# A list scheduler inside the kernel plans the order of all five queues

## Chip, core and metric

The kernel runs on one core of one Trainium2 chip. The core has five engines with a queue each: TensorE (PE), VectorE (DVE), ScalarE (ACT), GpSimd (POOL) and SyncE (SP), which issues all DMAs here. The metric is the device time of one execution in microseconds; the kernel before took 1773.93, 1771.78 and 1771.08 us in three runs, 1771.78 in the middle.

## What is computed

Two layers of a gated trunk on 640 token columns: 512 latent ones (modulated by `c`, attending to cached context and to themselves) and 128 context ones (modulated by `c_ctx`). Cut to the core, one layer of the reference is:

```python
shift, scale, gate = split(silu(c) @ w_mod + b_mod, 3)
h = rms(x, norm_g) * (1 + scale) + shift
cq, ckv, krope, z_a, qkv_b, ga, gb, z_b, cu, cv, z_c, gl = split(h @ w_in)
o_a = attention(rms(rms(cq) @ w_uq), keys_values(rms(ckv) @ w_ukv, krope))      # 8 heads
o_b = rms(gdn(silu(conv5(qkv_b)), ga, gb, forward) + gdn(..., backward))        # 4 heads, chunked scan
o_c = gelu(cu) * (w_s @ layernorm(gelu(cv)) + b_s)                              # per 128 positions
yb = [(o_a * silu(z_a)) @ w_b0, (o_b * silu(z_b)) @ w_b1, (o_c * silu(z_c)) @ w_b2]
x = x + gate * ((sigmoid(gl) * yb).sum() @ w_o)
```

Beside the two outputs it returns the new ckv, krope and states of the context.

## The kernel before

Activations lie feature-major: 128 features by 640 tokens, worked in two halves of 320 columns. The weights are streamed: a tile `raw` of 128x512 (256 KB, `wload`, L130) is split into a rounded part `hi` by ScalarE (L134) and the rest `lo` by VectorE (L135), and `dense` multiplies in three passes, L146 (hi by hi), L147 and L148 (the two mixed products), into PSUM tiles `dn` of two buffers. Small products go to `mm` (p1, two buffers) and `p2` (two buffers). SBUF tiles are cut from tags with a fixed number of slots (`NB`): `G` has 13, `raw`, `hi` and `lo` 3 each.

Four places matter below.

The start. `Mod.groups` loads the 128x512 tiles of w_mod into `G` (L205) and multiplies them with the two conditioning vectors (L208); after 16 tiles VectorE copies the sums to `mrow` (L210), TensorE transposes them (L213), and out of them come shift and scale of half the features. `make_h` makes with them four of the eight tiles `hh`, `hl` of h, and dense matmuls of layer 0 need these. Then the other 16 tiles follow for the other half. The constants of `late_constants` (L1148), a layer's vectors (`lvec`, L303) and b_mod and norm_g (L190, L192) are small loads.

The scans of the four heads of branch B. Each step multiplies a state, L533 and L534, VectorE corrects (L536), L500 multiplies again, ScalarE weights the result (L505), and L544 makes the state's update. L780 is the spatial product of the gated MLP (branch C), whose input `D` VectorE makes at L701.

The inverses of branch B: small tiled products of 32 and 64 rows in steps; the last joins are L670, L683 and L684.

Attention. `latent_tile` multiplies queries and keys (L1053 with 512 columns, L1054 with 128), `softmax` runs on VectorE and ScalarE (L1040 to L1046), five transpositions follow (L1059), ScalarE copies (L1061) and ten products of 64 rows (L1067) form the output. The preparation of the next pair of heads and the dense blocks of the other branches are laid between by generators.

The order of each queue is set before by the framework: it takes instructions in program order by priority, with its own cost model, and `tc.high_priority(HP)` lifts the splits, the evacuations of `dense`, the softmax and one normalisation above the rest:

```python
with tc.high_priority(HP):
    split_w(w[:, 0:n], hi[:, 0:n], lo[:, 0:n])
```

## Time and profile before

| what | value |
| --- | --- |
| three runs | 1773.93, 1771.78, 1771.08 us |
| span of the profiled execution | 1769.0 us |
| TensorE busy, matmuls | 1719.1 us (97%), 13422 |
| TensorE busy, weight loads | 1573.2 us (89%) |
| VectorE busy | 1075.1 us (61%) |
| ScalarE busy | 817.5 us (46%) |
| DMA, mean share of 16 engines' span | 26% |

The span is that of one profiled execution, and about 3 us shorter than the time of the middle run. Busy shares are means over a program with unlike stages. In the timeline an engine's idle time stands in brackets behind the instruction that ended it, with what released it. Matmuls of plain fp32 are recorded twice each, so that a count of 8 there is four matmuls; L146 to L148 once.

### The profile page before, as it was taken

What the parts mean: (1) busy time and instruction counts of PE and PEld (TensorE: products, weight loads), DVE (VectorE), ACT (ScalarE), POOL (GpSimd) and SP (SyncE); (2) the same over time, 40 slices, a digit from 0 to 9 for tenths busy, and PEclk for the clock granted to TensorE, in tenths of its full rate; (3) what the DMA queues carried; (4) which work ended last, traced back from release to release, by engine and by line L of the source; (5) the groups of instructions that cost most, each with busy time, mean ns of one, the idle gap of its engine ahead of it and who ended that gap; (6) DMA issues with size and microseconds to landing.
All of it is one profiled execution on the core that took longest, in us unless ns stands there. A gap on an engine that the chain in (4) does not pass through costs nothing.

```text
span 1769.0 us, 34645 instructions
## 1 busy us (share of the span) xinstructions
PE 1719.1 (97%) x13422; PEld 1573.2 (89%) x13422; DVE 1075.1 (61%) x3180; ACT 817.5 (46%) x2065; POOL 16.7 (1%) x100
## 2 busy tenths in 40 slices
PE   6999999999999999999999999999999999999999
PEld 3899988898888889999989989888988888899999
DVE  4798888565555643433559988885655656435352
ACT  3466764554544542222335666655544545323231
POOL 0000000000000000000000000000000000000000
PEclk9999999999999999999999999999999999999999
DMA  8211121221112242554432211111211112123224
GB/s 289 70 56 58 54 67 40 67 72 62 40 38 65 63 141 72 167 179 150 156 117 67 61 44 59 59 47 61 72 52 53 50 53 66 62 72 108 78 88 138
DMA packets 86421, 146.37 MB, mean 83 GB/s; under 512 B 14064, under 2 KB 21616, under 8 KB 86256
## 3 DMA queue, kind: packets, MB, share of 16 engines
q1 hardware_dynamic: 86256, 144.15, 26.0%
q8 instruction: 106, 1.74, 0.4%
q14 instruction: 59, 0.48, 0.1%
HBM read 132.28 MB, written 11.83 MB: 81 GB/s over the span
## 4 chain that ended last, share of the span: by engine, by line
PE 85%; DVE 7%; ACT 5%; issue 1%; DMA 1%; SPq 0%; ACTq 0%; DVEq 0%
PE dn L146 19%; PE dn L147 19%; PE dn L148 19%; PE p L1053 3%; PE mm L1067 3%; PE p L1059 2%; DVE C L332 2%; PE p L208 1%; PE mm L500 1%; PE p L147 1%; PE p L148 1%; DVE lo L135 1%; PE p L146 1%; PE mm L544 1%; ACT hi L134 1%
## 5 line engine op out<-in xcount | busy, mean ns | idle before, releaser
L146 PE MATMUL dn<-hh,hi 128*128 128x320 f32 (+1 forms) x2208 | 697.0, 316 | 5.4 <-ACT hh L268 4.9
L147 PE MATMUL dn<-hl,hi 128*128 128x320 f32 (+1 forms) x2208 | 693.0, 314 | 1.2 <-DVE hl L269 1.1
L148 PE MATMUL dn<-hh,lo 128*128 128x320 f32 (+1 forms) x2208 | 693.4, 314 | 0.0
L146 PEld LDWEIGHTS dn<-hh,hi 128*128 128x128 f32 (+1 forms) x2208 | 413.6, 187 | 16.9 <-ACT hh L268 5.9
L147 PEld LDWEIGHTS dn<-hl,hi 128*128 128x128 f32 (+1 forms) x2208 | 413.8, 187 | 6.4 <-DVE hl L269 2.6
L148 PEld LDWEIGHTS dn<-hh,lo 128*128 128x128 f32 (+1 forms) x2208 | 413.7, 187 | 3.7 <-issue 2.2
L135 DVE TENSOR_TENSOR lo<-raw,hi 128x512 fp32r<-128x512 f32 (+1 forms) x326 | 223.9, 688 | 217.6 <-ACT hi L134 212.8
L134 ACT CAST hi<-raw 128x512 fp32r<-128x512 f32 (+1 forms) x326 | 201.2, 619 | 316.6 <-PE dn L147 293.3
L146 PE MATMUL dn<-qkv,hi 128*128 128x320 f32 x384 | 119.7, 312 | 0.0
L147 PE MATMUL dn<-qkv,hi 128*128 128x320 f32 x384 | 119.4, 311 | 0.0
L148 PE MATMUL dn<-qkv,lo 128*128 128x320 f32 x384 | 118.9, 310 | 0.0
L821 ACT ACTIVATE th<-dn 128x320 f32<-128x320 f32 x96 | 41.6, 434 | 110.2 <-PE dn L148 109.8
L1040 DVE TENSOR_REDUCE mx<-p 128x1 f32<-128x640 f32 x64 | 52.6, 822 | 64.2 <-PE p L1054 64.2
L332 DVE SCALAR_TENSOR_TENSOR C<-C,l_conv_w,C 128x644 f32<-128x644 f32 x96 | 84.8, 883 | 5.2 <-ACT C L330 3.4
L1044 ACT ACTIVATE V<-p,mx,scl 128x640 f32<-128x640 f32 x64 | 56.6, 884 | 56.5 <-DVE mx L1042 43.1
L147 PEld LDWEIGHTS dn<-qkv,hi 128*128 128x128 f32 x384 | 72.1, 188 | 0.7 <-issue 0.7
L146 PEld LDWEIGHTS dn<-qkv,hi 128*128 128x128 f32 x384 | 72.1, 188 | 0.7 <-issue 0.7
L148 PEld LDWEIGHTS dn<-qkv,lo 128*128 128x128 f32 x384 | 72.1, 188 | 0.0
L1061 ACT COPY V<-p 128x640 f32<-128x640 f32 x64 | 44.3, 692 | 53.1 <-PE p L1059 53.1
L1053 PE MATMUL p<-G,G 128*128 128x512 f32 x128 | 66.1, 598 | 0.0
L833 DVE SCALAR_TENSOR_TENSOR th<-th,dn 128x320 f32<-128x320 f32 x64 | 31.2, 487 | 44.6 <-PE dn L148 44.6
L1126 DVE SCALAR_TENSOR_TENSOR ya<-dn,gate,ld 128x320 f32<-128x320 f32 (+2 forms) x48 | 19.6, 437 | 54.8 <-DMA ld<-sp 23.0
(395 smaller groups left out, 2675.3 us busy)
## 6 DMA issues: line engine op xcount, KB each, us to landing
raw<-in_w_in SPq DMA_DIRECT2D x244, 256.0 KB, 2.6
G<-in_w_mod SPq DMA_DIRECT2D x96, 256.0 KB, 4.3
raw<-in_w_branch SPq DMA_DIRECT2D x48, 256.0 KB, 2.6
raw<-in_w_o SPq DMA_DIRECT2D x32, 256.0 KB, 2.6
ld<-sp SPq DMA_DIRECT2D x24, 320.0 KB, 3.2
G<-in_w_uq SPq DMA_DIRECT2D x16, 192.0 KB, 2.8
ya<-in_xT SPq DMA_DIRECT2D x8, 320.0 KB, 5.4
sp<-V SPq DMA_DIRECT2D x8, 320.0 KB, 2.5
```

The costliest lines, as they stand in the source:

```text
L134: S.copy(hi, w)
L135: V.tensor_tensor(lo, w, hi, ALU.subtract)
L146: PE.matmul(out, ah, bh, start=start, stop=False)
L147: PE.matmul(out, ah, bl, start=False, stop=False)
L148: PE.matmul(out, al, bh, start=False, stop=stop)
L332: V.scalar_tensor_tensor(cv, buf[:, w : w + 644], convw[:, j, w : w + 1], cv, ALU.mult, ALU.add)
L821: S.activation(ga[c0], acc, AF.Tanh, scale=0.5)
L1040: V.tensor_reduce(mx, src, AX.X, ALU.max)
L1044: S.activation(out, src, AF.Exp, scale=sc_, bias=mx[:, 0:1], accum_out=ls[:, 0:1])
L1053: PE.matmul(psS[:, 0:512], pr.qT[j][:, qs], pr.kT[j][:, 0:512], start=True, stop=True)
L1061: S.copy(pT.rearrange("p a b -> p (a b)"), pst[:, 0:640])
L1067: PE.matmul(po[es, 0:P], pr.Vt[:, kt, e, :] if kt < 4 else pr.Vc[:, e, :], PT[e][:, kt, :], start=(kt == 0), stop=(kt == 4), tile_position ...
```

## The change

Every engine call now goes to a `Recorder`, which notes the operation, the tiles it reads and writes (as sets of columns and partitions) and, from these, what it depends on. No instruction is issued while the program runs. At the end `rec.issue()` lets `plan()` run an event list over all operations: each engine takes, when it is free, the ready operation of lowest priority number (program order, less 100000 under `rec.hp()`); the slots of a tag are given out in program order; costs come from `cost()` and a few constants. Then it issues in the planned order, and each instruction is tied to the one before on its engine and to the last users of its slot. The same tiles and the same 16907 instructions result; the computation is unchanged. In the order after, all rows have the line L330, where `issue()` calls the engine.

```diff
+ENG = {"V": "vector", "S": "scalar", "G": "gpsimd", "PE": "tensor", "SP": "sync"}
+
+TAIL = {"V": 80, "S": 95, "G": 60}
+HOP = {"V": 60, "S": 60, "G": 100, "PE": 60, "SP": 60}
+SLACK = 150
+ISSUE = 55
+DMA_LAG, DMA_RATE = 1900, 250.0
...
+class Recorder:
+
+
+    def __init__(self, tc):
+        self.tc, self.ops, self.off = tc, [], 0
+        self.acc = {}
+        self.tag = {}
+        self.users = {}
+        self.boxes = {}
+        self.rows = {}
...
+    def add(self, eng, meth, args, kw):
+        op = Op()
+        op.n, op.eng, op.meth, op.args, op.kw = len(self.ops), eng, meth, args, kw
+        op.prio = op.n - self.off
+        op.preds, op.succs, op.tiles = set(), [], []
...
+    def cost(self, op, outs, ins):
+        size = lambda x: x.free_size() if callable(x.free_size) else x.free_size
+        e = op.eng
+        op.ld = 0
+        if e == "SP":
+            big = max((x.nbytes() if callable(x.nbytes) else x.nbytes) for x in outs + ins)
+            op.occ, op.lat = ISSUE, big / DMA_RATE
+        elif e == "PE":
+            n = size(outs[0])
+            if op.meth == "transpose":
+                op.ld, op.occ = 107, max(n / 2.4, 64) + 2
+            elif ins[0].dtype == F32R:
+                op.ld, op.occ = 107, n / 2.4 + 13
+            else:
+                rows = ins[0].ap[0][1]
+                op.ld, op.occ = (107, 4 * n / 2.4 + 4) if rows > 64 else (40, 4 * n / 2.4 + 4)
+                if rows > 64:
+                    op.occ = max(op.occ, 120)
+            op.lat = op.occ + 180
+        else:
+            n = max(size(x) for x in outs[:1] + ins[:1])
+            ps = any(self.tag.get(x.tensor.name, ("", False, 0))[1] for x in outs + ins)
+            if e == "V":
+                quick = op.meth in ("tensor_scalar", "tensor_copy", "memset") and not ps
+                d = max(160, 150 + (0.63 if quick else 1.05 * (1 if not ps else 1.0)) * n)
+                if op.meth == "reciprocal":
+                    d = max(160, 150 + 2 * n)
+            elif e == "S":
+                d = max(230, 165 + 0.88 * n) + (190 if "accum_out" in op.kw else 0)
+            else:
+                d = 200 + 1.2 * n
+            op.occ, op.lat = d - TAIL[e], d
...
+        def slots_ok(op, t):
+            for nm in op.tiles:
+                if nm in home:
+                    continue
+                tag = self.tag[nm][0]
+
+                if nxt[tag] != pos[nm] or not any(f[0] <= t for f in free[tag]):
+                    return tag
+            return None
...
+            for s_ in op.succs:
+                s_.left -= 1
+                lag = 0.0
+                if s_.eng != op.eng or op.eng == "SP":
+                    lag = HOP[s_.eng] + (SLACK if s_.eng == "PE" else 0)
+                elif op.eng == "PE":
+                    lag = -1e6
+                s_.ready = max(s_.ready, op.end + lag)
+                if s_.left == 0:
+                    post(s_.ready, "rdy", s_)
+
+        def dispatch(e, t):
+            h = avail[e]
+            if busy[e] > t:
+                return
...
+    def issue(self):
+        out = self.plan()
+        self.rank = {op.n: i for i, op in enumerate(out)}
+        nc = self.tc.nc
+        deps = {}
+        for op, nm in self.slotdeps:
+            deps.setdefault(op.n, []).append(nm)
+        prev = {}
+
+        def behind(op, other, why):
+            info = mybir.DependencyInfo(mybir.DependencyClass.NoSync, mybir.DependencyReason.DATA)
+            self.tc.add_manual_dep(op.ins.ins, other.ins.ins.name, info, reason=why)
+
+        for op in out:
+            op.ins = getattr(getattr(nc, ENG[op.eng]), op.meth)(*op.args, **op.kw)
+            if op.eng in prev:
+                behind(op, prev[op.eng], "order")
+            prev[op.eng] = op
+            for nm in deps.get(op.n, ()):
+                lastof = {}
+                for u in self.users[nm]:
+                    if u.eng not in lastof or self.rank[u.n] > self.rank[lastof[u.eng].n]:
+                        lastof[u.eng] = u
+                for u in lastof.values():
+                    if u.eng != op.eng:
+                        behind(op, u, "slot")
...
+class RecHigh:
+    def __init__(self, rec):
+        self.rec = rec
+
+    def __enter__(self):
+        self.rec.off += HP
+
+    def __exit__(self, *x):
+        self.rec.off -= HP
...
-    V, S, G, PE = nc.vector, nc.scalar, nc.gpsimd, nc.tensor
+    rec = Recorder(tc)
+    V, S, G, PE, SY = (rec.engine(e) for e in ("V", "S", "G", "PE", "SP"))
...
-        nc.sync.dma_start(w[:, 0 : src.shape[1]], src)
+        SY.dma_start(w[:, 0 : src.shape[1]], src)
...
-        with tc.high_priority(HP):
+        with rec.hp():
...
+    rec.issue()
```

All other edits replace `nc.sync` by `SY`, `tc.high_priority` by `rec.hp()` and drop comments.

**At the start, SP's queue**: before, the last of the first 16 w_mod tiles (`G`, of which G_58 is the sixteenth), three raw weights and the next w_mod tiles. The names are tile names with a running number.

```order
L205 DMA G_56_223<-in_w_mod 128x512
L205 DMA G_57_227<-in_w_mod 128x512
L205 DMA G_58_231<-in_w_mod 128x512
L130 DMA raw_73_279<-in_w_small 128x384
L130 DMA raw_76_285<-in_w_in 128x512
L130 DMA raw_79_291<-in_w_in 128x512
L205 DMA G_83_298<-in_w_mod 128x512
L205 DMA G_84_302<-in_w_mod 128x512
```

And after, from the twelfth tile on; between l_gdn and l_kn_rope stand 32 more small loads, which are left out:

```order
L330 DMA G_54_122<-in_w_mod 128x512
L330 DMA G_55_123<-in_w_mod 128x512
L330 DMA raw_73_141<-in_w_small 128x384
L330 DMA raw_76_144<-in_w_in 128x512
L330 DMA raw_79_147<-in_w_in 128x512
L330 DMA l_conv_w_113_181<-in_conv_w 128x60
L330 DMA l_gdn_onorm_114_182<-in_gdn_onorm 128x1
...
L330 DMA l_kn_rope_3060_3128<-in_kn_rope 128x32
L330 DMA G_56_124<-in_w_mod 128x512
L330 DMA G_57_125<-in_w_mod 128x512
L330 DMA G_58_126<-in_w_mod 128x512
L330 DMA G_83_151<-in_w_mod 128x512
```

The 14th to 16th tile (G_56 to G_58) now come behind the raw weights and 35 small loads.

**TensorE's queue at the same place**, before: `p2_36` collects the first half, `p2_82` the second, mm_60 is the transposition, dn_117 and p2_119 the first dense blocks.

```order
L208 MATMUL p2_36_135<-G_57_227,c_s32_13_84 32x256 x2
L208 MATMUL p2_36_135<-G_58_231,c_s32_13_84 32x256 x2
L213 MATMUL mm_60_237<-c_ident_2_69,mrow_59_235 128x128 x2
L208 MATMUL p2_82_297<-G_83_298,c_s32_13_84 32x256 x2
L146 MATMUL dn_117_415<-hh0_62_244,hi_74_281 48x320
L146 MATMUL p2_119_417<-hh0_62_244,hi_77_287 128x320
L208 MATMUL p2_82_297<-G_84_302,c_s32_13_84 32x256 x2
```

And after:

```order
L330 MATMUL p2_36_104<-G_57_125,c_s32_13_81 32x256 x2
L330 MATMUL p2_36_104<-G_58_126,c_s32_13_81 32x256 x2
L330 MATMUL p2_82_150<-G_83_151,c_s32_13_81 32x256 x2
L330 MATMUL mm_60_128<-c_ident_2_68,mrow_59_127 128x128 x2
L330 MATMUL p2_82_150<-G_84_152,c_s32_13_81 32x256 x2
L330 MATMUL p2_82_150<-G_85_153,c_s32_13_81 32x256 x2
L330 MATMUL p2_82_150<-G_86_154,c_s32_13_81 32x256 x2
L330 MATMUL dn_117_185<-hh0_62_130,hi_74_142 48x320
L330 MATMUL dn_118_186<-hh0_62_130,hi_74_142 48x320
```

Four tiles of the second half (G_83 to G_86) are multiplied before the first dense matmul, where one was.

**TensorE in a head's scan**, before: mm_764 and mm_770 are L533 and L534 of two steps, mm_766 is L500, mm_768 L544, dn_842 an L780.

```order
L533 MATMUL mm_764_3776<-Q_757_3759,qkv_418_2046 128x128
L534 MATMUL mm_764_3776<-Q_757_3759,qkv_406_1966 128x128
L780 MATMUL dn_842_4092<-C_807_3913,D_590_2807 128x128
L500 MATMUL mm_766_3782<-Q_765_3779,G_728_3610 128x128
L544 MATMUL mm_768_3787<-Q_767_3784,G_458_2276 128x128
L533 MATMUL mm_770_3791<-Q_763_3774,qkv_418_2046 128x128
L534 MATMUL mm_770_3791<-Q_763_3774,qkv_406_1966 128x128
```

And after, from mm_766 to mm_770:

```order
L330 MATMUL mm_766_834<-Q_765_833,G_728_796 128x128
L330 MATMUL dn_838_906<-hl7_112_180,hi_834_902 128x320
L330 MATMUL dn_838_906<-hh7_111_179,lo_835_903 128x320
L330 MATMUL dn_840_908<-C_807_875,D_578_646 128x128
L330 MATMUL dn_840_908<-C_807_875,D_581_649 128x128
L330 MATMUL dn_840_908<-C_807_875,D_584_652 128x128
L330 MATMUL dn_840_908<-C_807_875,D_587_655 128x128
L330 MATMUL mm_768_836<-Q_767_835,G_458_526 128x128
L330 MATMUL mm_770_838<-Q_763_831,qkv_418_486 128x128
L330 MATMUL mm_770_838<-Q_763_831,qkv_406_474 128x128
```

Two dense matmuls (dn_838) and four L780 (dn_840) have moved between mm_766 and mm_768.

**TensorE in a softmax join**, before: p2_1184 is the score product, p2_1188 the transposition of its softmax, and 23 dense matmuls stand between (five are shown).

```order
L1053 MATMUL p2_1184_5693<-G_1104_5353,G_1075_5195 128x512
L1054 MATMUL p2_1184_5693<-iv_1102_5343,G_1075_5195 128x128
L146 MATMUL dn_1546_7283<-qkv_1478_6895,hi_1544_7279 128x320
L147 MATMUL dn_1546_7283<-qkv_1479_6897,hi_1544_7279 128x320
L148 MATMUL dn_1546_7283<-qkv_1478_6895,lo_1545_7280 128x320
...
L146 MATMUL dn_1554_7323<-hh0_62_244,hi_1549_7313 128x320
L147 MATMUL dn_1554_7323<-hl0_63_245,hi_1549_7313 128x320
L1059 MATMUL p2_1188_5704<-c_ident_2_69,V_1185_5696 128x128 x5
```

And after, with nine L1067 (mm_1172) and twelve products of 256 columns (mm_1183) between, of which some are shown:

```order
L330 MATMUL p2_1184_1252<-G_1104_1172,G_1075_1143 128x512
L330 MATMUL p2_1184_1252<-iv_1102_1170,G_1075_1143 128x128
L330 MATMUL mm_1172_1240<-V_1171_1239,G_1088_1156 64x128
L330 MATMUL mm_1172_1240<-V_1165_1233,G_1088_1156 64x128
L330 MATMUL mm_1172_1240<-V_1171_1239,G_1088_1156 64x128
...
L330 MATMUL mm_1172_1240<-V_1171_1239,Q_1089_1157 64x128
L330 MATMUL mm_1183_1251<-G_1174_1242,C_1031_1099 128x256
L330 MATMUL mm_1183_1251<-G_1175_1243,C_1031_1099 128x256
...
L330 MATMUL mm_1183_1251<-G_1174_1242,iv_1063_1131 128x256
L330 MATMUL p2_1188_1256<-c_ident_2_68,V_1185_1253 128x128 x5
```

The dense matmuls have moved away, and shorter products stand in their place.

## Rows read from the trace of the kernel before

**Rows 1.** The page, parts 1 and 4: busy us (share); chain by engine.
```profile
PE 1719.1 (97%) x13422; PEld 1573.2 (89%) x13422; DVE 1075.1 (61%) x3180; ACT 817.5 (46%) x2065; POOL 16.7 (1%) x100
...
PE 85%; DVE 7%; ACT 5%; issue 1%; DMA 1%; SPq 0%; ACTq 0%; DVEq 0%
```

**Rows 2.** Windows: PE, PEld, DVE, ACT, POOL busy us; clock, DMA share, GB/s.
```profile
0.00:60.00 60.00, 41.44 (x239) 23.53 (x240) 26.05 (x67) 18.32 (x33) 0.54 (x10) 0.91 0.68 228
60.00:260.00 200.00, 197.15 (x1732) 184.87 (x1730) 173.92 (x613) 129.63 (x390) 6.61 (x40) 1.00 0.20 59
260.00:400.00 140.00, 132.76 (x1283) 121.77 (x1284) 98.45 (x334) 74.89 (x218) 1.25 (x3) 1.00 0.20 63
905.00:935.00 30.00, 26.97 (x212) 21.85 (x210) 22.22 (x59) 12.78 (x23) 0.17 (x3) 0.94 0.21 65
1130.00:1270.00 140.00, 132.40 (x1266) 120.79 (x1264) 97.34 (x336) 75.35 (x219) 2.05 (x5) 0.99 0.19 62
1540.00:1769.00 229.00, 225.20 (x1535) 224.85 (x1534) 92.85 (x166) 59.62 (x109) 0.00 (x0) 1.00 0.31 97
```

**Rows 3.** Timeline of SP, start: start us, duration us, line, operation.
```profile
7.18 12.78 SPq L205 DMA_DIRECT2D G<-in_w_mod  x16
20.01 0.42 SPq L130 DMA_DIRECT2D raw<-in_w_small  x1
...
21.48 12.11 SPq L205 DMA_DIRECT2D G<-in_w_mod  x16
```

**Rows 4.** Timeline of SP, 62.5 to 70 us: small loads back to back.
```profile
65.65 0.42 SPq L303 DMA_DIRECT2D l_kv_a_norm<-in_kv_a_norm  x1
...
68.97 0.43 SPq L303 DMA_DIRECT2D l_a_log<-in_a_log  x1
```

**Rows 5.** The page, part 6: count, KB, us from issue to landing.
```profile
raw<-in_w_in SPq DMA_DIRECT2D x244, 256.0 KB, 2.6
```

**Rows 6.** Timeline of PE, start: in brackets idle us before, releaser.
```profile
27.76 0.44 PE L213 MATMUL mm<-c_ident,mrow 128*128 128x128 f32 x2 [0.57 <-DVE mrow L210]
...
31.03 0.63 PE L208 MATMUL p<-G,c_s 128*32 128x256 f32 x4
```

**Rows 7.** Timeline of PE, 294 to 299 us: a head's scan.
```profile
294.25 1.05 PE L780 MATMUL dn<-C,D 128*128 128x128 f32 x8
...
296.69 0.49 PE L500 MATMUL mm<-Q,G 128*128 128x128 f32 x2 [0.22 <-DVE Q L536]
297.70 0.49 PE L544 MATMUL mm<-Q,G 128*128 128x128 f32 x2 [0.52 <-ACT Q L505]
```

**Rows 8.** Line L544: waits before it, by releaser (us, times).
```profile
  ACT Q L505: 8.3, 33
```

**Rows 9.** Line L780: waits before it, by releaser (us, times).
```profile
  DVE D L701: 7.6, 12
```

**Rows 10.** Timeline of PE, 463 to 468 us: one softmax join.
```profile
463.61 0.38 PE L1054 MATMUL p<-iv,G 128*128 128x128 f32 x2
463.75 0.40 PE L146 MATMUL dn<-qkv,hi 128*128 128x320 f32 x1
...
467.06 0.31 PE L147 MATMUL dn<-hl,hi 128*128 128x320 f32 x1
467.29 0.77 PE L1059 MATMUL p<-c_ident,V 128*128 128x128 f32 x5
```

**Rows 11.** Timeline of DVE, 463 to 468 us: the softmax's last step.
```profile
466.68 0.55 DVE L1046 TENSOR_SCALAR V<-V,ls 128x640 f32<-128x640 f32 x1
```

**Rows 12.** Timeline of PE, 454 to 464 us: L1067 and 256-column products.
```profile
459.38 0.98 PE L1067 MATMUL mm<-V,G 128*64 128x128 f32 x13
...
460.62 0.39 PE L147 MATMUL mm<-G,C 128*128 128x256 f32 x1
...
462.63 0.28 PE L148 MATMUL mm<-G,iv 128*128 128x256 f32 x1
```

**Rows 13.** Line L1059: largest wait before it (us, times).
```profile
  issue: 4.6, 16
```

More of the change, by code (lines that the diff above doesn't have):

```diff
@@ L45, with __init__, __getattr__ @@
+class RecEngine:
+    def __init__(self, rec, e):
+        self.rec, self.e = rec, e
+    def __getattr__(self, meth):
+        return lambda *args, **kw: self.rec.add(self.e, meth, args, kw)
+class RecHigh:
[5 more added lines that the diff above has]
+        self.rec.off -= HP
 class Kern:
@@ L62, in T @@
         kw = {} if bufs is None else {"bufs": bufs}
-        return (pool or sb).tile(shape, dt, tag=tag, name=f"{tag}_{uid[0]}", **kw)
+        t = (pool or sb).tile(shape, dt, tag=tag, name=f"{tag}_{uid[0]}", **kw)
+        return rec.tile(t, tag, pool is ps, shape, bufs or (2 if pool is lay or pool is None else 1))
     def pdense():
@@ L91, in dbg @@
         if dump and name in dump:
-            nc.sync.dma_start(dump[name], t)
+            SY.dma_start(dump[name], t)
     def cload(name, shape):
         t = T(shape, "c_" + name, pool=const)
-        nc.sync.dma_start(t, a[name])
+        SY.dma_start(t, a[name])
         return t
@@ L156, in dense @@
                 mm3(acc[0:m, 0:HF], wh, wl, xh[k][:, cs], xl[k][:, cs], k == 0, k == len(wk) - 1)
-            with tc.high_priority(HP):
+            with rec.hp():
                 evac(acc[0:m, 0:HF], hf * HF, hf * HF + HF)
@@ L176, in run @@
             for (wk, m, evac), ac in zip(blocks, acc):
-                with tc.high_priority(HP):
+                with rec.hp():
                     for hf in range(2):
@@ L189, in __init__ @@
             self.bm = T([P, 24], "bmod", pool=lay)
-            nc.sync.dma_start(self.bm, a["b_mod"][l])
+            SY.dma_start(self.bm, a["b_mod"][l])
             self.ng = T([P, KM], "normg", pool=lay)
-            nc.sync.dma_start(self.ng, a["norm_g"][l])
+            SY.dma_start(self.ng, a["norm_g"][l])
             self.raw = T([P, 24, 2], "mod", pool=lay)
@@ L204, in groups @@
                     w = X("G", [P, 512])
-                    nc.sync.dma_start(w, a["w_mod"][self.l, g, k])
+                    SY.dma_start(w, a["w_mod"][self.l, g, k])
                     for h in range(2):
@@ L286, in spill @@
         d_ = dram.tile([P, NT], F32, tag=f"sp{uid[0]}", name=f"sp{uid[0]}")
-        nc.sync.dma_start(d_, t)
+        rec.tile(d_, f"sp{uid[0]}", False, [P, NT], 1)
+        SY.dma_start(d_, t)
         return d_
@@ L302, in lvec @@
             t = T(shape, "l_" + name, pool=lay)
-            nc.sync.dma_start(t, a[name][l] if src is None else src)
+            SY.dma_start(t, a[name][l] if src is None else src)
             return t
@@ L733, in layer @@
         next(gd[1], None)
-        with tc.high_priority(HP):
+        with rec.hp():
             vnt = []
@@ L759, in layer @@
         wsT = X("C", [P, 4, P])
-        nc.sync.dma_start(wsT, a["w_sT"][l])
+        SY.dma_start(wsT, a["w_sT"][l])
         bsb = X("C", [P, 512])
-        nc.sync.dma_start(bsb, a["b_s"][l].partition_broadcast(P))
+        SY.dma_start(bsb, a["b_s"][l].partition_broadcast(P))
         lng = lvec("cm_ln_g", [P, 4])
@@ L807, in branch @@
                     u = X("ld", [P, NT])
-                    nc.sync.dma_start(u, f)
+                    SY.dma_start(u, f)
                     f = silu_block((B_ZA, B_ZB)[n] + q, "C")
@@ L906, in layer @@
         V.tensor_scalar(nck, pt[:, 0:256], rkv[:, 4:5], None, ALU.mult)
-        nc.sync.dma_start(o["new_ckv"][l], nck)
+        SY.dma_start(o["new_ckv"][l], nck)
         cch = T([P, 2, P], "iv", bufs=NB["iv"])
-        nc.sync.dma_start(cch, a["cache_ckvT"][l])
+        SY.dma_start(cch, a["cache_ckvT"][l])
         cchh = T([P, 2, P], "iv", F32R, bufs=NB["iv"])
@@ L1036, in softmax @@
         def softmax(src, n, pr, j, t, out):
-            with tc.high_priority(HP):
+            with rec.hp():
                 mx = T([P, 1], "mx1", bufs=3)
@@ L1119, in layer @@
             xo = X("ld", [P, NT])
-            nc.sync.dma_start(xo, xsrc[m])
+            SY.dma_start(xo, xsrc[m])
             xn = T([P, NT], f"ya{m}", bufs=1)
@@ L1129, in layer @@
             if last:
-                nc.sync.dma_start(o["y"][:, m, :], xn)
+                SY.dma_start(o["y"][:, m, :], xn)
             else:
@@ L1139, in trunk_kernel @@
         xt[k] = T([P, NT], f"ya{k}", bufs=1)
-        nc.sync.dma_start(xt[k], a["xT"][:, k, :])
+        SY.dma_start(xt[k], a["xT"][:, k, :])
     mods.append(Mod(0))
```

185 lines of the change are left out of this document (178 added, 7 removed).

## The prediction

> **What bounds the kernel now.** I read the shares of busy time and the chain that ended last first. TensorE is busy for 1719.1 of 1769.0 us, 97%, its weight loads for 89%, and 85% of the chain is TensorE's, VectorE having 7% and ScalarE 5% [rows 1]. The change leaves all matmuls, tiles and transfers as they are and only reorders them, so it can win or lose nothing but time in which TensorE stands. The table by stage says where that is [rows 2]: TensorE's busy time is short of the stretch by 60.0 - 41.44 = 18.56 us in the first 60 us, by 2.85 in the next 200, by 7.24 in the head scans and spatial gating of layer 0 (260 to 400), by 3.03 at the start of layer 1 (905 to 935), and by 7.60 in layer 1's scans (1130 to 1270). The profile's total is 1769.0 - 1719.1 = 49.9, so 49.9 - 18.56 = 31.3 lie outside the first 60 us. The last stretch, 1540 to 1769, has 229.0 - 225.20 = 3.8 of them [rows 2], which I leave to the output projection and the last stores; what an order could win after the start is 31.3 - 3.8 = 27.5 us. So a planner has at most about 1.6% to win, and the first question is whether it keeps what the old order had.
>
> **Start: w_mod loads.** Before, SP issues the 16 w_mod tiles of the first half back to back, from 7.18 us over 12.78 us (0.80 each), then three raw weights from 20.01 to 21.48, then the second 16 [rows 3]. The new order puts 13, then the three raws, then 35 small loads (conv_w, masks, cos, the vectors of both layers), and only then tiles 14 to 16. It does so because 13 is the number of G slots, and at the moment when the 14th waits for a slot the planner lets anything else pass, at a price of 55 ns each. The trace has another price: eight DMAs of this kind in a row show seven steps from 65.65 to 68.97, 3.32 / 7 = 0.47 us each [rows 4]. So SP reaches tile 14 at 7.18 + 13 x 0.80 + 1.47 + 35 x 0.47 = 35.5 us, issues the 16th at 35.5 + 2 x 0.47 = 36.4 (the queue is empty by then, so the issue price holds), and it lands 2.6 later [rows 5] at 39.0. With its matmuls (0.63) and VectorE's copy (0.57 of wait before L213, and some 0.3 for the hop on either side) the transposition L213 starts at about 40.5, where it started at 27.76 [rows 6]: +12.7. The first group's vectors gate h, and h gates every dense matmul of layer 0. While it waits, TensorE can pull ahead only what stands before the first dense matmul: L208 on four tiles of the second group instead of one, three more at 0.63 each or somewhat over [rows 6], 2 to 2.4. Net +10.5. Bounds: at half the price per small load (0.24, if they overlap) +2.5; at the 0.80 that a w_mod tile takes [rows 3], if each small load had to wait behind as much, 35 x 0.33 = 11.5 more, +22.
> The Trainium skill, "DMA: Bandwidth & Descriptors", section "Issuing engines are not separate DMA queues", says that the time on the sequencer to start a DMA "is usually small relative to the DMA itself"; by that rule, and the planner's 55 ns, 35 small loads cost about 2 us and the start stays as it was. The trace disagrees: 0.47 us of SP for each [rows 4] against 2.6 for a 256 KB tile [rows 5], so the measurement decides; the rule is kept as rival 2.
>
> **Scans.** Each step of a head's scan goes L533, VectorE, L500, ScalarE, L544. Before, L500 waits 0.22 us and L544 right behind it 0.52 with nothing between [rows 7]; L544's waits come to 8.3 us in 33 [rows 8]. Now six products stand between at the same place, two dense (0.15 each) and four of L780, which took 1.05 us together [rows 7]: 1.35 us cover a wait of 0.52. Not each of the 48 steps gets this, and cover given here is missing from another; I take half, -4 (bounds 0 and -8.3). L780, which read D late, waited 7.6 us in 12 [rows 9]; the new order starts D's chain earlier and has more dense work ahead of it. I take -5 (0 to -7.6).
>
> **Attention.** A score product (L1054) is followed by the softmax on VectorE and ScalarE and then by five transpositions (L1059). Before, at the place shown, L1054 starts at 463.61 and L1059 at 467.29, with 23 dense matmuls between, 3.31 / 22 = 0.15 each [rows 10]; the last step of the softmax ends at 466.68 + 0.55 = 467.23 [rows 11]. So 3.68 us are needed from start to start, and dense work fills all but 0.2. Now nine 64-column products (L1067) and twelve 256-column ones stand there. Nine took 460.62 - 459.38 = 1.24 us, and the others (462.63 - 460.62) / 16 = 0.126 each [rows 12], twelve 1.51. Together 2.75 against 3.68 - 0.14 = 3.54: a new wait of 0.8 us. The planner sees none, since it prices a 64-column product at 4 x 128 / 2.4 + 4 = 217 ns, where the row gives 1.24 / 9 = 138. In the two layers 10 of 64 such places are so thin: 10 x 0.8 = 8. The other 54 have more cover than before by about 0.4 us in the middle, which takes 5 of the waits that L1059 had, the largest of which is put down to issue, 4.6 us in 16 [rows 13]. Net +3 (-8 to +9).
>
> **Inverses.** In front of the joins of the 64-wide inverses the order leaves nine dense matmuls where thirteen stood, 4 x 0.15 = 0.6 us less, eight times: 0 to +4.8. The row has no large wait there before, so the old cover was about sufficient; I take +3.
>
> **Layer 1's start.** Of the 3.03 us of idle in 905 to 935 [rows 2] the new order can fill about half with w_mod products: -1.5 (0 to -3). The semaphore waits get fewer and the order edges within an engine add no instruction, so here is no loss; the gain is at most the chain's 1% of issue [rows 1], some 18 us, and I take 0, since R1 holds that end.
>
> **Sum.** +10.5 - 4 - 5 + 3 + 3 - 1.5 = +6.0 us on the profiled span of 1769.0; around the span lie 1771.78 - 1769.0 = 2.8 us between it and the median of the runs. 1769.0 + 6.0 + 2.8 = 1777.8, so 1778 us. A difference under 0.2% (1768.2 to 1775.3) is no change that can be measured here.
>
> **Rivals.**
> R1, the planner closes the gaps: all 27.5 us of idle after the start go, because it knows each engine's latency and holds 150 ns (SLACK) in reserve for each edge onto TensorE. For it: VectorE's 7% and ScalarE's 5% of the chain [rows 1] are joins of the kind a list scheduler hides, and the scan place does get cover. Against: the thin softmax join, and 27.5 is the whole of it. 1769.0 + 10.5 - 27.5 + 2.8 = 1754.8, so 1755 us, faster.
> R2, the small loads cost the start nothing, because SP's 0.47 us per load lies beside the landing of the 13 tiles before them: tiles 14 to 16 come as before, the four early L208 save 1 us. 1769.0 - 1 - 4.5 + 2.8 = 1766.3, so 1766 us: the sum's other terms, -4 - 5 + 3 + 3 - 1.5 = -4.5. For it: 13 tiles are under way when the small loads begin. Against: 35 x 0.47 = 16.5 us of SP, more than the whole 12.78 that 16 tiles took [rows 3]. The rule of the Trainium skill named above would have it come out so.
> R3, thin joins in the scans: the planner's short latency for ScalarE leaves each of the 48 L500 to L544 hops with the wait of 0.52 that the row has when nothing is between [rows 7]. 48 x 0.52 = 25.0, against 8.3 before [rows 8]: +16.7. It decides as soon as most hops hold less than 0.5 us of other work, that is fewer than three dense matmuls. 1769.0 + 10.5 - 5 + 16.7 + 2.8 = 1794.0, slower. Against it: the place shown has 1.35 us.
>
> **Chances and range.** Forecast 0.45, of which 0.37 lies above 1775.3 and 0.08 within 0.2%. R1 0.27, all faster. R2 0.13: 0.08 faster and 0.05 the same. R3 0.15, slower. So faster 0.35, same 0.13, slower 0.52. The forecast's own range is 1768 to 1790, from the bounds of the start (-8, and +11.5) with the joins' terms as taken. To hold eight in ten the range must take in most of R1 and R3: 1752 to 1794.
>
> **What would show it.** Start: L213 first at about 40 us instead of 27.76, SP's small loads from 19 us to 35 with 0.47 us each, and TensorE's busy time in the first 60 us down to about 31. Scans: L544's waits for ScalarE near 4 us, L780's for VectorE near 2.6. Attention: about ten waits of 0.6 to 1.0 us before the L1059 transpositions, put down to VectorE's last softmax step. The prediction is wrong if tile 14 leaves SP before 25 us, or if busy time in 260 to 400 and in 1130 to 1270 fills the stretch to within 1 us.

## The result, and the profile after

The changed kernel takes 1795.56 us (median of four runs, 1793.49 to 1797.23) against 1772.51 us for the kernel before in the same job: ratio 1.0131, 95% interval 1.0117 to 1.0145. The forecast was 1778, with a range up to 1794: the side was right, the size was not, and the range ended 1.6 us short of the measurement.

The page after, part 1: busy time of each engine.

```profile
PE 1716.5 (96%) x13422; PEld 1579.9 (88%) x13422; DVE 1083.3 (60%) x3180; ACT 813.5 (45%) x2065; POOL 16.6 (1%) x100
```

TensorE has the same work as in [rows 1], 1716.5 us against 1719.1, in a span of 1795.4 us: it stands 78.9 us instead of 49.9, and all of the loss is time in which TensorE stands or runs at the low clock. (The mean granted clock is 0.990 against 0.995; of 1795 us that is an estimate of 9 us, part of it while TensorE stood anyway.) The table by stage says where (columns as in [rows 2]; the stages have moved by up to 26 us, so only the idle time in a row is to be compared):

```profile
0.00:60.00 60.00, 35.50 (x192) 17.23 (x192) 19.57 (x57) 13.92 (x24) 0.37 (x7) 1.00 0.70 229
60.00:260.00 200.00, 191.08 (x1689) 179.04 (x1688) 171.59 (x585) 124.28 (x367) 4.91 (x39) 0.99 0.18 54
260.00:400.00 140.00, 127.10 (x1247) 117.39 (x1246) 98.33 (x328) 75.65 (x232) 3.08 (x6) 0.99 0.20 57
400.00:660.00 260.00, 258.39 (x1832) 230.95 (x1832) 150.12 (x440) 124.50 (x287) 0.00 (x0) 0.99 0.21 65
...
935.00:1130.00 195.00, 184.40 (x1642) 171.87 (x1635) 165.53 (x569) 119.17 (x350) 4.79 (x36) 0.98 0.18 52
1130.00:1270.00 140.00, 128.48 (x1244) 118.01 (x1243) 98.79 (x325) 73.54 (x224) 3.25 (x9) 0.96 0.19 55
```

Idle time of TensorE is 24.5 us in the first 60 us (18.56 before), 8.9 in the next 200 (2.85), 12.9 in the scans of layer 0 (7.24), 10.6 in 935 to 1130 (195 - 184.40), which holds the end of layer 1's start (2.3 before), 11.5 in the scans of layer 1 (7.60); in attention, 400 to 660, it is 1.6 (2.15).

Since the stages move, a clock of work is better than a clock of time. I matched every matmul of a run with its counterpart of before, gave each the same fixed price (columns / 2.4 + 13.5 ns for the dense ones, four times the columns / 2.4 for plain fp32, times the share of the array that it uses; 1633.8 us in all) and read from each trace when so much work had been done. The second column is the time in the kernel before, the others are how much later (us) the other kernels got there; the experiments are those of the next section.

```
work done   before | after   SP waits   L208 price   small tiles   all prices of PE   all corrections
  40          80.3 |  11.5     -2.7         9.5          10.3            9.4               -3.4
 165         211.6 |  11.5     -2.8         9.4           9.3            7.9               -7.2
 320         396.1 |  20.6      7.8        20.8          13.4           16.8               -4.2
 640         719.1 |  15.4      2.2        15.8           8.9            9.2               -5.0
 820         902.3 |  17.5      4.3        15.7          10.9            9.1               -5.1
 840         929.7 |  25.3     10.9        14.8          18.2            7.4               -6.9
 980        1075.6 |  25.5     11.1        15.7          17.0            7.8               -9.6
1200        1330.4 |  29.7     13.4        20.0          15.2            8.7               -7.2
1630        1761.2 |  26.4     10.2        17.1          12.1            3.8              -11.1
```

In the column "after": 11.5 us are lost at the start, 9.1 in the scans and inverses of layer 0 (165 to 320), 5.2 come back in attention, 2.1 are lost at the gate vectors, 7.8 at the start of layer 1 (820 to 840), 4.2 in layer 1's scans and inverses, and 3.3 come back in its attention.

**The start.** SP's queue after (start us, duration us, line, operation):

```profile
7.96 7.83 SPq L330 DMA_DIRECT2D G<-in_w_mod  x13
...
18.41 0.33 SPq L330 DMA_DIRECT2D l_conv_w<-in_conv_w  x1
...
36.13 0.43 SPq L330 DMA_DIRECT2D l_kn_rope<-in_kn_rope  x1
36.68 7.09 SPq L330 DMA_DIRECT2D G<-in_w_mod  x13
```

These rows answer to [rows 3]: 35 small loads stand from 18.41 to 36.68 where the second 16 tiles stood; (36.68 - 18.41) / 35 = 0.52 us each. Only then does tile 14 leave. TensorE's queue in the same time:

```profile
28.77 1.94 PE L330 MATMUL p<-G,c_s 128*32 128x256 f32 x16
40.76 3.18 PE L330 MATMUL p<-G,c_s 128*32 128x256 f32 x16 [10.05 <-DMA G<-in_w_mod]
43.87 0.69 PE L330 MATMUL mm<-c_ident,mrow 128*128 128x128 f32 x2
...
46.63 0.64 PE L330 MATMUL dn<-hh,hi 128*48 128x320 f32 x2 [0.79 <-ACT hh L330]
```

After its thirteenth tile TensorE waits 10.05 us for the fourteenth; L213, the transposition, starts at 43.87, where [rows 6] had 27.76.

**The start of layer 1.** TensorE's queue:

```profile
932.62 4.44 PE L330 MATMUL mm<-G,c_s 128*32 128x256 f32 x42
...
938.49 0.31 PE L330 MATMUL p<-hl,hi 128*128 128x320 f32 x1
943.85 0.69 PE L330 MATMUL mm<-c_ident,mrow 128*128 128x128 f32 x2 [5.05 <-DVE mrow L330]
...
944.87 0.47 PE L330 MATMUL dn<-hl,hi 128*48 128x320 f32 x1
```

And VectorE's:

```profile
935.32 1.93 DVE L330 SCALAR_TENSOR_TENSOR hl<-qkv,mod,hh 128x512 fp32r<-128x512 f32 x4
...
942.72 0.74 DVE L330 SCALAR_TENSOR_TENSOR hl<-qkv,mod,hh 128x512 fp32r<-128x512 f32 x1
943.38 0.42 DVE L330 COPY mrow<-mm 128x256 f32<-128x256 f32 x1
```

The w_mod products (L208) end at 937.06, but the copy to mrow that the transposition needs starts at 943.38: on VectorE it stands behind make_h's operations on four of the eight tiles of h and part of those on two more. On TensorE the transposition stands in front of dense matmuls that ran right behind it without a wait. 5.05 us of wait come first, and then the low clock. The windows around it (columns as in [rows 2]):

```profile
929.20:936.00 6.80, 5.81 (x42) 3.80 (x46) 3.34 (x11) 2.45 (x5) 0.00 (x0) 0.50 0.35 124
...
938.50:943.80 5.30, 0.30 (x3) 0.04 (x1) 5.30 (x13) 3.32 (x8) 0.00 (x0) 0.91 0.00 0
944.20:949.40 5.20, 5.20 (x21) 4.36 (x20) 4.83 (x14) 1.94 (x4) 0.17 (x3) 0.50 0.00 0
949.80:960.00 10.20, 10.20 (x72) 9.22 (x71) 2.44 (x5) 1.81 (x4) 0.00 (x0) 1.00 0.08 26
```

VectorE is busy for all 5.30 us of the wait. Behind it the granted clock is 0.50, that is 1.2 GHz, for 5.2 us, where a dense matmul's record is 0.47 us long instead of 0.31 and the step to the next 0.27 us instead of 0.15; then it is 1.00 again. An earlier stretch at 0.50, 929.2 to 936.0, lies under the w_mod products.

**Scans and inverses.** TensorE's timeline after, two joins of one inverse (L664, then L683):

```profile
226.62 0.84 PE L330 MATMUL p<-iv,iv 32*32 32x32 f32 x60 [1.08 <-ACT iv L330]
...
230.47 1.15 PE L330 MATMUL p<-iv,G 64*64 64x64 f32 x20 [1.06 <-DVE iv L330]
```

And some 50 us later the transpositions of a finished head's output (L573) and of the next head's preparation (L476):

```profile
277.30 1.65 PE L330 MATMUL mm<-c_ident,V 128*128 128x128 f32 x5 [2.84 <-ACT V L330]
...
284.42 0.74 PE L330 MATMUL p<-c_ident,qkv 128*128 128x128 f32 x5 [1.61 <-DVE qkv L330]
```

L664 waited 4.0 us in all before and waits 7.7 now (all eight inverses), L683 0.0 and now 4.0; L573 0.9 and now 5.0, L476 0.0 and now 4.0. The waits of the scan itself changed little: L500 0.4 to 2.0, L544 1.3 to 1.2, L780 3.3 to 1.2. All these are TensorE's idle time ahead of matmuls, from the two traces, matmul by matmul.

**Attention.** TensorE's timeline after at the join of [rows 10]:

```profile
482.13 0.38 PE L330 MATMUL p<-iv,G 128*128 128x128 f32 x2
...
485.77 0.77 PE L330 MATMUL p<-c_ident,V 128*128 128x128 f32 x5 [0.40 <-DVE V L330]
```

From L1054 to L1059 it takes 3.64 us, 3.68 before; the wait is 0.40.

### The profile page after: what moved, and what is told of

It is laid out like the page before. It is cut to its first block, busy times and chain, and to the rows that moved or that the text cites. A ratio compares the mean times of both kernels' runs of the same rounds, so it can differ in the third digit from the quotient of the medians.

```text
span 1795.4 us, 34588 instructions
## 1 busy us (share of the span) xinstructions
PE 1716.5 (96%) x13422; PEld 1579.9 (88%) x13422; DVE 1083.3 (60%) x3180; ACT 813.5 (45%) x2065; POOL 16.6 (1%) x100
## 5 line engine op out<-in xcount | busy, mean ns | idle before, releaser
L330 PE MATMUL dn<-hh,hi 128*128 128x320 f32 (+1 forms) x2208 | 699.0, 317 | 5.3 <-ACT hh L330 2.4
L330 PE MATMUL dn<-hl,hi 128*128 128x320 f32 (+1 forms) x2208 | 694.4, 315 | 0.6 <-DVE hl L330 0.6
L330 PE MATMUL dn<-hh,lo 128*128 128x320 f32 (+1 forms) x2208 | 694.4, 315 | 0.0
L330 PEld LDWEIGHTS dn<-hh,hi 128*128 128x128 f32 (+1 forms) x2208 | 415.0, 188 | 18.3 <-issue 3.8
L330 PEld LDWEIGHTS dn<-hl,hi 128*128 128x128 f32 (+1 forms) x2208 | 415.6, 188 | 4.2 <-DVE hl L330 1.3
L330 PEld LDWEIGHTS dn<-hh,lo 128*128 128x128 f32 (+1 forms) x2208 | 415.1, 188 | 4.8 <-issue 2.9
L330 DVE TENSOR_TENSOR lo<-raw,hi 128x512 fp32r<-128x512 f32 (+1 forms) x326 | 225.0, 692 | 244.2 <-ACT hi L330 238.4
L330 ACT CAST hi<-raw 128x512 fp32r<-128x512 f32 (+1 forms) x326 | 201.1, 619 | 339.9 <-PE dn L330 317.8
L330 PE MATMUL dn<-qkv,hi 128*128 128x320 f32 x768 | 176.0, 312 | 0.0
L330 ACT ACTIVATE th<-dn 128x320 f32<-128x320 f32 x176 | 76.4, 434 | 133.3 <-PE dn L330 132.8
L330 PEld LDWEIGHTS dn<-qkv,hi 128*128 128x128 f32 x768 | 128.8, 188 | 1.9 <-issue 1.4
L330 PE MATMUL dn<-qkv,lo 128*128 128x320 f32 x384 | 119.5, 311 | 0.0
L330 DVE SCALAR_TENSOR_TENSOR C<-C,l_conv_w,C 128x644 f32<-128x644 f32 x96 | 85.0, 886 | 7.0 <-ACT C L330 5.4
L330 DVE TENSOR_REDUCE mx<-p 128x1 f32<-128x640 f32 x64 | 52.7, 823 | 60.4 <-PE p L330 60.4
L330 ACT ACTIVATE V<-p,mx,scl 128x640 f32<-128x640 f32 x64 | 56.7, 886 | 55.5 <-DVE mx L330 44.8
L330 ACT COPY V<-p 128x640 f32<-128x640 f32 x64 | 44.3, 693 | 70.9 <-PE p L330 70.9
L330 PE MATMUL mm<-V,G 128*64 128x128 f32 (+1 forms) x672 | 74.7, 281 | 0.2
L330 PEld LDWEIGHTS dn<-qkv,lo 128*128 128x128 f32 x384 | 72.2, 188 | 0.7 <-issue 0.7
L330 DVE SCALAR_TENSOR_TENSOR th<-th,dn 128x320 f32<-128x320 f32 x96 | 46.6, 486 | 41.2 <-PE dn L330 38.0
L330 PEld LDWEIGHTS p<-iv,G 32*32 32x32 f32 (+2 forms) x608 | 34.5, 131 | 40.4 <-issue 33.2
L330 PEld LDWEIGHTS mm<-V,G 128*64 128x64 f32 (+1 forms) x672 | 55.5, 149 | 12.8 <-issue 8.9
L330 PE MATMUL p<-G,G 128*128 128x512 f32 x128 | 65.4, 593 | 0.0
```

The source lines that it names most:

```text
L330: op.ins = getattr(getattr(nc, ENG[op.eng]), op.meth)(*op.args, **op.kw)
```

## The experiments

All are the changed kernel with an edit of the planner's numbers or of one of its rules; tiles, instructions and computation stay, and `issue()` calls the engine from L330 to L333. Times are medians, the ratio is to the kernel before in the same job.

**1. SP does not pass a blocked w_mod tile.**

```diff
                     blocked.setdefault(tag, []).append(op)
+                    if e == "SP" and tag == "G" and t < 40000:
+                        return
                     continue
```

> The planner's SP does not pass a w_mod tile that waits for a G slot in the first 40 us of its plan, so that all 32 w_mod tiles and the three raw weights stand before the small loads, as in the kernel before; prices as in the changed kernel. If the small loads are what delays the start: first L213 at 27 to 29 us, the 11.5 us lost by 80 us of the old run gone, all later losses as they were: 1782 to 1786. Rival, TensorE is bound at the start by something else (price of w_mod products, order on TensorE): under half of it, 1789 to 1793.

Measured 1782.40 us, ratio 1.0064 (1.0047 to 1.0081), 12 to 13 us less than the changed kernel. SP's queue in this kernel:

```profile
7.77 10.54 SPq L332 DMA_DIRECT2D G<-in_w_mod  x16
...
20.67 15.44 SPq L332 DMA_DIRECT2D G<-in_w_mod  x16
36.17 0.42 SPq L332 DMA_DIRECT2D l_conv_w<-in_conv_w  x1
```

And TensorE's first transposition and first dense matmul:

```profile
31.50 0.44 PE L332 MATMUL mm<-c_ident,mrow 128*128 128x128 f32 x2 [0.53 <-DVE mrow L332]
...
34.01 0.34 PE L332 MATMUL dn<-hh,hi 128*48 128x320 f32 x1 [1.51 <-ACT hh L332]
```

L213 starts at 31.50, later than the 27 to 29 expected but 12.4 earlier than in the changed kernel, and from work 40 on the column "SP waits" runs 13 to 16 us below "after" throughout: the start's loss is the small loads', and nothing behind it takes it back. By work 40 this kernel is even 2.7 us ahead of the kernel before, although its first transposition comes 3.7 us later: its granted clock is 1.00 in the first 77 us, where the kernel before has 0.94 in the first 80.

**2. The price of a DMA alone.** `ISSUE = 55` becomes 470.

> The planner's price of a DMA on SP goes from 55 to 470 ns, nothing else. In the new order six small loads, not 35, stand before the 14th w_mod tile. If the start's loss comes from SP's time on small loads: 29 x 0.47 = 13.6 us less before tile 14, the first L213 at 30 to 31 us instead of 43.9, and about 11 us back of the 26.4 that the changed kernel loses on TensorE's work: 1784 to 1786. The rest (start of layer 1, scans) stays. Rival, the start is bound by the landing of tiles and the loss returns elsewhere: 1793 to 1796.

Measured 1791.64 us, ratio 1.0122 (1.0105 to 1.0139). Neither range was met. Tile 14 left SP at 22.42 and L213 started at 32.55, so the start is mended in great part; the profiled run, the fastest of the four (1787.87 to 1793.20), is 9.3 us ahead of the changed kernel's at the end. But the median is only 4 us lower, and as ratios 1.0122 and 1.0131 with overlapping intervals are not to be told apart. SP's queue shows that small loads still stand between the w_mod tiles, up to 44 us; that this is what makes a right price alone worth less than the rule of experiment 1 is likely and not shown by itself, and why the four runs differ by 5 us is open.

**3. All TensorE prices.**

```diff
             if op.meth == "transpose":
-                op.ld, op.occ = 107, max(n / 2.4, 64) + 2
+                op.ld, op.occ = 107, 110
...
-                op.ld, op.occ = (107, 4 * n / 2.4 + 4) if rows > 64 else (40, 4 * n / 2.4 + 4)
-                if rows > 64:
-                    op.occ = max(op.occ, 120)
+                share = rows / 128 * min(size(ins[0]), 128) / 128
+                op.ld = 107 if rows > 64 else 40
+                op.occ = max(4 * n / 2.4 * share + 4 * share, 223 if n == 1 else 58 if rows > 32 else 14)
```

> The planner's prices of TensorE products go to what the trace shows: 32-column products 107 instead of 431 ns, 64-column ones 107 instead of 217, 32x32 ones 14 instead of 57, 64x64 ones 58 instead of 111, 128x128 transpositions 110 instead of 66, single-column products 223 instead of 120; DMA price as it was. Theory 'prices': the VectorE copy before L213 at the start of layer 1 stood behind make_h because w_mod products were priced four times too high; with right prices it moves 15 places ahead and the 5 us of wait go, with the low clock behind it: about -8 us, and half of what the scans and inverses lost in the two layers (9 and 8) comes back: 1778 to 1783, the first 60 us unchanged. Theory 'latency' (VectorE and ScalarE are priced 3 to 4% too short): only the 8 us at layer 1: 1786 to 1789. If neither, 1793 to 1798.

Measured 1772.61 us, ratio 1.0014 (1.0005 to 1.0024): 21 us back, more than either theory gave. The start of layer 1 no longer loses (9.1 to 7.4 between work 820 and 840), and layer 1's scans lose 0.9 instead of 4.2; layer 0's still lose 8.9.

**4. The 32-column price alone** (L208 at 107 ns instead of 431).

> Only the price of the 32-column w_mod products (L208) goes from 431 to 107 ns. The copy to mrow moves from row 1553 of VectorE to row 1534, ahead of make_h. If that price alone makes the loss at the start of layer 1: the wait of 5.05 us before the transposition and the low clock behind it go, 7 to 10 us: 1785 to 1789; scans and inverses of layer 1 lose their 8 us as before. If right prices of the small tiles were needed too: 1792 or more.

Measured 1787.70 us, ratio 1.0095 (1.0078 to 1.0113). TensorE's queue at the start of layer 1:

```profile
930.66 1.06 PE L332 MATMUL mm<-G,c_s 128*32 128x256 f32 x12
932.89 0.44 PE L332 MATMUL mm<-c_ident,mrow 128*128 128x128 f32 x2 [1.18 <-DVE mrow L332]
```

And VectorE's:

```profile
931.49 1.01 DVE L332 SCALAR_TENSOR_TENSOR qkv<-ya,scale,C 128x512 f32<-128x512 f32 x2 [2.20 <-ACT C L332]
932.42 0.41 DVE L332 COPY mrow<-mm 128x256 f32<-128x256 f32 x1
```

The copy runs at 932.42, 0.7 us after the last w_mod products end (931.72) and behind two operations of make_h instead of twenty-one, and the transposition waits 1.18 us instead of 5.05. Between work 820 and 840 the kernel gains 0.9 us on the kernel before, where the changed one lost 7.8; each other stage of the table is within 2.4 us of "after". So this loss is the price of L208.

**5. The prices of 32- and 64-row products alone** (the inverses: 14 and 58 ns instead of 57 and 111).

> Only the prices of products on 32 and 64 rows (the inverses) go to 14 and 58 ns, from 57 and 111. If the joins of the inverses are thin because the planner counts 160 + 160 + 4 x 80 such products as cover that they are not: waits at L664 and L683, 11.7 us together, fall to about 5, and the scans after them gain: 1783 to 1789. If the loss in the scans has another origin (the late inputs of head 3 and z): 1791 to 1797. The start of layer 1 keeps its wait of 5 us in both cases.

Measured 1782.99 us, ratio 1.0071 (1.0057 to 1.0085): 10 to 11 us back. TensorE's timeline at an inverse of layer 0 (L664, L683):

```profile
292.66 0.84 PE L332 MATMUL p<-iv,iv 32*32 32x32 f32 x60 [1.69 <-ACT iv L332]
...
296.24 0.33 PE L332 MATMUL p<-iv,G 64*64 64x64 f32 x2 [0.29 <-DVE iv L332]
```

And its largest wait around layer 1's scans (L466):

```profile
1152.86 2.03 PE L332 MATMUL p<-qkv,qkv 128*128 128x128 f32 x10 [3.54 <-ACT junk L332]
```

Between work 165 and 320 the loss falls from 9.1 to 4.1, between 980 and 1200 from +4.2 to -1.8; L683 waits 1.5 us in all instead of 4.0, L476 not at all, L573 2.3 instead of 5.0. L664 hardly changed (7.2), and a new wait of 3.54 stands before L466. (The expectation's 160 + 160 + 4 x 80 are records, two to a product.) So with this price the loss goes, but not at the join that I had named first. That the small products' phantom time on TensorE made the plan believe in cover that was not there, and so brought late inputs around the heads' ends, fits the waits that went (L683, L476, L573); I did not follow it in the plan. In layer 0 this price is not all: experiment 3, which has it right too, still loses 8.9 there.

**6. VectorE and ScalarE 4% longer**, `d *= 1.04` ahead of the line that sets `op.occ, op.lat`.

> The planner's durations of VectorE and ScalarE operations are all made 4% longer, which is what the trace has in the mean (1222.7 us against 1188.1 planned on VectorE, 904.7 against 870.4 on ScalarE); all else as changed. Theory 'latency': TensorE's queue reaches the joins of the scans and inverses before their input, since the plan has the input too early; with right durations 12 to 17 us come back: 1779 to 1784. Theory 'prices': within 3 us of the changed kernel, 1793 to 1798.

Measured 1782.79 us, ratio 1.0067 (1.0052 to 1.0082). That looks like the theory 'latency', until it is put on top of right TensorE prices (below).

**7. Both prices** (2 and 3 together).

> Both the DMA price (470 ns) and the TensorE prices of the trace; VectorE and ScalarE as changed. If the two causes add: -11 at the start and -8 to -17 elsewhere, 1767 to 1777, equal to the kernel before or a little better. If the start's gain is given back behind it: 1780 or more.

Measured 1768.26 us, ratio 0.9990 (0.9981 to 0.9999): by the ratios 25 us back, against 2 and 21 for the two alone, so within the noise the causes add.

**8. All corrections** (1, 2, 3 and 6).

> All together: DMA price 470 ns, TensorE prices of the trace, VectorE and ScalarE 4% longer, and SP not passing a blocked w_mod tile at the start. If the causes add beyond the kernel with both prices (1768.3): start another 2 to 3 us and scans 2 to 5: 1759 to 1766, faster than before. If the lengthened durations only shuffle the scans: 1765 to 1771.

Measured 1759.80 us, ratio 0.9937 (0.9923 to 0.9950): faster than both kernels, by 10 us than the one before. Part 1 of its page:

```profile
PE 1708.3 (97%) x13422; PEld 1583.9 (90%) x13422; DVE 1076.5 (61%) x3180; ACT 810.6 (46%) x2065; POOL 16.8 (1%) x100
```

Its windows in the scans (columns as in [rows 2]):

```profile
260.00:420.00 160.00, 151.85 (x1377) 142.01 (x1376) 105.82 (x391) 78.46 (x226) 1.23 (x3) 0.95 0.19 55
...
1130.00:1290.00 160.00, 152.04 (x1377) 141.99 (x1376) 103.56 (x376) 78.36 (x221) 0.99 (x2) 0.95 0.20 57
```

Beside them the same windows of the changed kernel:

```profile
260.00:420.00 160.00, 146.92 (x1383) 136.95 (x1382) 112.05 (x384) 83.50 (x249) 3.08 (x6) 0.98 0.21 61
1130.00:1290.00 160.00, 148.48 (x1380) 137.77 (x1379) 113.77 (x381) 87.58 (x261) 3.25 (x9) 0.96 0.20 59
```

In the two scan stages TensorE stands 8.2 and 8.0 us instead of 13.1 and 11.5, but its granted clock is lower there too, 0.95 in both against 0.98 and 0.96. Where does the gain of 10 us on the kernel before lie? Not in idle time: TensorE stands 1757.9 - 1708.3 = 49.6 us in all, as it did before (49.9). It lies in busy time, 1708.3 us against 1719.1, and that although the mean granted clock is 0.988 against 0.995. A dense matmul's record (0.31 us) outlasts the step to the next one (0.15), so a wait of up to 0.16 us behind it counts as busy. From a matmul of 320 or 256 columns to a product of another kind the step, idle time left out, is 216 ns in the mean before (479 such steps) and 190 ns here (470): 103.7 us against 89.4 in all.

**9. The same without the 4%.**

> DMA price, TensorE prices and SP waiting for a blocked w_mod tile; VectorE and ScalarE durations as in the changed kernel. It splits the gain of the kernel with all corrections (1759.8) over the one with both prices (1768.3). If the start made it: 1760 to 1763. If the 4% made it: 1765 to 1768.

Measured 1761.70 us, ratio 0.9941 (0.9926 to 0.9956), not to be told from 0.9937. With right TensorE prices and the start mended, the durations of VectorE and ScalarE are worth nothing more in sum. Nor do they save idle time in the scans, where this kernel stands 9.2 and 6.1 us:

```profile
260.00:420.00 160.00, 150.83 (x1397) 140.44 (x1397) 108.57 (x375) 80.03 (x231) 1.00 (x2) 0.97 0.19 58
1130.00:1290.00 160.00, 153.92 (x1416) 144.16 (x1417) 109.42 (x383) 78.77 (x230) 1.00 (x2) 0.97 0.18 56
```

By the marks of the table they seem to move the loss: between work 165 and 320 this kernel loses 8.0 us and that of experiment 8 3.0, and between 320 and 640 this one wins 7.7 and that one 0.8. But mark 320 (391.9 us in the kernel of 8) lies inside a stretch at the low clock that is far shorter in this kernel. In the kernel of 8, at the end of layer 0's heads, and then the windows there and at the same place of layer 1:

```profile
387.31 1.65 PE L333 MATMUL mm<-c_ident,V 128*128 128x128 f32 x5 [1.76 <-ACT V L333]
```

```profile
388.30:402.00 13.70, 13.03 (x59) 12.50 (x60) 5.68 (x39) 2.23 (x6) 0.00 (x0) 0.50 0.13 44
1255.30:1269.00 13.70, 13.11 (x60) 12.68 (x60) 5.67 (x39) 2.10 (x5) 0.00 (x0) 0.50 0.14 45
```

Behind a wait of 1.76 us for the transpositions of the last head the granted clock is 0.50 for 13.7 us, and half of that, 6.9 us as an estimate, is lost; this kernel's clock is 0.88 between 385 and 399 us. The 10.1 us of the stretch behind the mark cost some 5 us that the table books under attention, and with them layer 0 loses as much in 8 as here. What holds the clock down there, no run isolates. So the 4% that brought 11 us back in 6 bring nothing beside right TensorE prices.

**10 to 12. More margin.** `SLACK = 350` on the changed kernel; the same on all corrections; and 8% instead of 4%.

> The reserve on every edge onto TensorE (SLACK) goes from 150 to 350 ns, prices wrong as in the changed kernel. If what counts is only the margin in front of TensorE's joins, this does what longer VectorE and ScalarE durations did: 1780 to 1786. If the prices count (TensorE ahead of its plan by several us in the inverses, which 0.2 us per edge does not catch): 1790 to 1797. Start and start of layer 1 lose as before in both.

> All corrections and SLACK 350. If margin still pays after the prices are right: 1754 to 1758. If 150 was enough: 1758 to 1764.

> All corrections, but VectorE and ScalarE 8% instead of 4% longer than the changed kernel's prices. If accuracy is what counts: the same or worse than 4%, 1759 to 1766. If more margin is better: 1753 to 1758.

Measured 1802.09 us (ratio 1.0168, 1.0153 to 1.0183), 1776.31 (1.0021, 1.0012 to 1.0031) and 1765.65 (0.9961, 0.9947 to 0.9976). The first two came out slower than both of their ranges, the third in that of accuracy. Margin makes each of them slower: SLACK 350 by 7 us on the changed kernel and by 15 on all corrections, the 8% by some 4, which is at the edge of what the intervals tell. With all corrections and SLACK 350, the transpositions L573 alone wait 22.7 us, 3.9 without.

## Why the prediction was wrong

**What bounds.** Right in the main: TensorE's work did not change; its idle time grew by 29.0 us while its busy time, which holds the clock and the short waits of experiment 8, fell by 2.6.

**Start, +10.5.** Right in mechanism: +11.5 by work 40, tile 14 leaving SP at 36.68 instead of the 35.5 worked out. That the net is so close is partly luck, for L213 came 16.1 us later, not 12.7. 13 tiles took 7.83 us, not 10.4, and a small load 0.52, not 0.47; TensorE went on 4.1 us after tile 14 was issued, not 2.6. For this last I had taken the row of `raw`, and the page of before has one for the w_mod tiles themselves:

```profile
G<-in_w_mod SPq DMA_DIRECT2D x96, 256.0 KB, 4.3
```

What made up for it, beside the w_mod products pulled ahead, is a term that the sum does not have: behind its own waits at the start the kernel before ran at the low clock, and the changed one has 1.00 in its first 60 us.

```profile
31.60:38.40 6.80, 6.74 (x25) 2.76 (x23) 6.23 (x15) 3.56 (x7) 0.00 (x0) 0.50 0.88 309
```

6.8 us at half the clock are worth some 3.4. R2 fell: 35 small loads held SP for 18.3 us, and experiment 1 gives 12 to 13 us for taking them out of the way. The Trainium skill ("DMA: Bandwidth & Descriptors", section "Issuing engines are not separate DMA queues") says that starting a DMA is usually small against the DMA itself, and for each load that holds here too: 0.52 us of SP against 1.7 us or more until it lands in this trace. The prediction was wrong to say that the trace disagrees with it; what failed is R2's inference that many such starts in one queue cost nothing.

**Layer 1's start, -1.5.** This step failed: +7.8. I counted the idle time that w_mod products could fill, on TensorE alone, and did not look where the new order puts the copy on VectorE on which L213 waits. The order shows it: the copy stands behind make_h, because the planner prices an L208 at 4 x 256 / 2.4 + 4 = 431 ns, and the trace of before had the price in a row that I did not use:

```profile
24.82 2.37 PE L208 MATMUL p<-G,c_s 128*32 128x256 f32 x40
```

Two records are one product: 20 products in 2.37 us, 0.12 each. I found this error of price for L1067 and not for L208. Experiment 4 shows it.

**Scans -4, L780 -5, inverses +3; together -6.** This failed too: +9.1 in layer 0 and +4.2 in layer 1. First, the terms -4 and -5 were sized on rows that count two engines. [Rows 8] and [rows 9] hold the waits of matmuls and of weight loads together. Asked for L544's matmuls alone, and then for its weight loads alone, the trace of before says (releaser: us, times):

```profile
  ACT Q L505: 1.2, 3
```

```profile
  ACT Q L505: 7.1, 30
```

So 7.1 of the 8.3 us were waits of weight loads, beside which TensorE's matmuls may run on, and 1.2 were idle time of the matmuls. (Short waits hide in the steps between records, too. From a matmul of 320 or 256 columns to an L500, L522 or L544 that reads `Q`, 116 steps were 4.6 us longer in all than at 147 ns each before, and 111 are 3.6 us longer after. So somewhat more than 1.2 could be won, and about 1 was.) Of L780's 7.6 it was 3.3, of which 2.1 were won. Second, what I took as unchanged, the transpositions at the end of one head and before the next, now has late inputs (L573, L476). The inverses' own waits grew by 7.7 us, beyond my bound of 4.8, which counted only the cover of one join. Experiment 5 shows the price of the small products behind all of layer 1's loss and half of layer 0's. The other half is not settled: with all TensorE prices right layer 0 still loses 8.9 or 8.0 us (3 and 9), and the 3.0 of experiment 8 are no better, since its mark cuts a stretch at the low clock. Attention after it takes part of it back.

**Attention, +3.** Wrong sign: -5.2 and -3.3. At the thin join the need was right (3.64 against 3.68) and the wait half of what I had (0.40 against 0.8); but the 64 joins together wait 2.0 us where they waited 3.5, and with the short waits hidden in the records more: from the matmul in front to the first transposition they took 9.1 us more than 64 steps of 147 ns before, and 3.7 after. These 5.4 us are most of the 8.5 that the two layers' attention gave back; the rest I did not follow. I had given the thin tenth of the joins more weight than the other nine tenths.

**R1 and R3.** R3's number, 1794, came close for a reason that does not hold: the hops L500 to L544 are not thin. R1 was wrong for this kernel. With prices that the trace gives the planner does beat the old order, by 0.6%, and 1759.8 us is near R1's 1755; but that too is a number for another reason, since R1 had the late start left in and all later idle time gone, and experiment 8 has the start mended and as much idle time as before. Whether a planner wins was the wrong question; whether its prices are those of the trace was the right one.
